# A third buffer for raw weights, and VectorE in place of a DMA for some of the weight rests

## The chip, the cores and the metric

The kernel runs on one core of one Trainium2 chip. The metric is device time in microseconds (us) of one execution. The kernel before takes 2480.88 us, the median of three runs (2478.66 to 2480.95).

## The reference, cut to what matters

Two blocks of two layers each, in float32, on 512 tokens of 1024 features. The first block mixes tokens with differential attention and a gated linear recurrence, then has a feed-forward part (1024 to 4096 and back) and a gated projection of a second input. The second block mixes with pooling and an attention that keeps the 128 best keys by an index score, and then has a feed-forward part with a norm before and behind it:

```
h = rms_norm_2(x, g_pre_ffn[l])
f = jnp.square(jax.nn.relu(h @ w_ff1[l])) @ w_ff2[l]
x = x + rms_norm_2(f, g_post_ffn[l])
```

All weights come from HBM, each is used once. Most of the time goes into products of activations with weights.

## The kernel before, in words

**Split operands.** TensorE multiplies a rounded float type (`F32R`). To keep float32's accuracy each operand is split into a rounded part (the high part, `wh` for a weight) and the rest (`wl` = raw - `wh`), and each product becomes three: high by high, high by rest, rest by high. So a piece of weights passes three stations before TensorE can use it: a load from HBM to a raw tile, a rounding copy to the high tile, and the making of the rest.

**Pieces and their order.** `_plan` lists the pieces of all weights in the order of use. A piece is 128 partitions by 1024 elements, 512 KB: two blocks of 128 rows by 512 columns. The index weights come in smaller pieces (`wx`).
- `w_load` (line 185) asks for a `raw` tile and issues the load on SyncE. There are two raw buffers. SyncE has nearly nothing but these loads in its queue; a load waits there until the splits of the piece that had the buffer have read it.
- `w_conv` (line 192) splits the next piece. ScalarE makes the high part (L205). The rest is made in one of three ways. VectorE subtracts (the `else`). POOL subtracts, in two halves (L218: pieces 1 to 3 of the plan, and the index pieces of the second layer). Or ScalarE copies raw with the sign turned (L211) and POOL issues a DMA (L214) that reads the piece from HBM a second time and adds it to what stands in the tile: minus raw, rounded to the tile's type, plus raw. That last way is used for the weights named in `ON_POOL` from the plan's piece 4 on, and for those in `BY_DMA`.
- `w_ahead` (line 225) keeps the splits up to `LC` = 3 pieces ahead of the piece in use. In each turn of its loop it makes one split and then, if the load counter is less than `LD - LC` ahead of the split counter, one load. `take` calls it before each piece is used.

Piece 0 is split in halves ahead of all this. The high and rest tiles have four buffers each (`wh`, `wl`), which TensorE gives back piece by piece.

**Kept pieces.** In the second block some pieces are used more than once, by `gemm_h`, which works on the two halves of the tokens (256 each) one behind the other so that the norm of the first half can start early. Such pieces are put in tiles of their own by `keep_in`, in the pool `F` of 16 tiles that the feed-forward part also uses for its 16 hidden activations `Fs`. Two sets matter here. At the start of the part, the four pieces of `w_ff1_2` with columns 0 to 511 go into tiles that are free. At its end, the last product (`w_ff2_2`, columns 512 to 1023, rows from 2048 on) does its first 8 row blocks for both halves at once; the other 8, the four pieces k = 24, 26, 28 and 30, are kept for both halves, and their eight tiles are those of the hidden activations that TensorE has just finished with. Both sets are in `BY_DMA`.

**What sets the order.** Each engine works through its own list in order. The lists are planned before the run: program order is the priority, parts marked `urgent` go first, and an instruction is listed when the planner expects its inputs and a free tile. At run time semaphores hold an instruction until both are there, and everything behind it on that engine waits too. TensorE's list is written out by hand in program order. Its instructions and VectorE's pass through the wrapper `Lane`, so all of them show as line L130. Where the second block's norms begin, TensorE has a small product `ones` by `acc` (L130), which sums squares over features. ScalarE's squares (L420) and VectorE's or POOL's adds into `acc` feed it. POOL computes the inverse root (L406), and `bcast` (L444) spreads it.

**Scratch.** `dynamic_dma_scratch_size` sets aside 8 KB of each partition for the descriptors of POOL's DMAs.

The lines that the prediction's steps touch are these: L190 (loads), L205, L211, L214, L218 and the `else` of `w_conv` (splits), `hooks` in `block2` and `mlp` (norms), and `scales` in `mix1` (the first norm's inverse root `v`, on POOL).

Of the kernel before, what the change touches and what calls it, by code (L numbers as in the profile page):

```python
# [8 lines left out]
F32 = mybir.dt.float32  # L9
F32R = mybir.dt.float32r  # L10
# [15 lines left out]
PC = 1024  # L26
ORDER = {"w_out": (4, 5, 6, 7, 0, 1, 2, 3), "w_out_2": (2, 3, 0, 1, 4, 5, 6, 7)}
NX = 11
# [2 lines left out]

URGENT = 250

LD, LC, LH = 4, 3, 4
IDX_SCALE = 8 ** -0.5
ALL = slice(0, 512)
HALVES = (slice(0, 256), slice(256, 512))
# [21 lines left out]
def _plan():  # L59

    plan = []

    def grp(name, l, n0, k0, nk, step, w):
        for k in range(k0, k0 + nk, step):
            plan.append((name, l, n0, k, step, w))

    def mlp(a, b, l):
        for half in range(2):
            for g in range(4):
                grp(a, l, half * 2048 + g * 512, 0, 8, 2, 512)  # L70
            for g in range(2):
                grp(b, l, g * 512, half * 16, 16, 2, 512)

    for l in range(DEPTH):
        for n0 in (1536, 0, 512, 1024):
            grp("w_in", l, n0, 0, 8, 2, 512)
        for n0 in (2048, 2304):
            grp("w_in", l, n0, 0, 8, 4, 256)
        for n0 in range(0, D, 512):
            grp("w_out", l, n0, 0, 4, 2, 512)  # L80
        for g in range(2):
            grp("w_out", l, g * 512, 4, 4, 2, 512)
        mlp("w_mlp_in", "w_mlp_out", l)
        for g in range(2):
            grp("w_ple_proj", l, g * 512, 0, 2, 2, 512)
            grp("w_ple_gate", l, g * 512, 0, 8, 2, 512)
    for l in range(DEPTH):

        for k0, nk in ((0, 4), (4, 4)) if l == 0 else [(k, 2) for k in range(0, 8, 2)]:
            for n0, w in ((0, 256), (256, 328)):  # L90
                grp("index", l, n0, k0, nk, 2, w)
        for n0 in (512, 1024, 1536):
            grp("w_in_2", l, n0, 0, 8, 2, 512)
        for n0 in (256, 0):
            grp("w_in_2", l, n0, 0, 8, 4, 256)
        for n0 in range(0, D, 512):
            grp("w_out_2", l, n0, 0, 4, 2, 512)
        for g in range(2):
            grp("w_out_2", l, g * 512, 4, 4, 2, 512)
        mlp("w_ff1_2", "w_ff2_2", l)  # L100
    return plan


PLAN = _plan()

BY_DMA = [e for e in PLAN if e[0] == "w_ff1_2" and e[2] in (0, 512) or e[0] == "w_ff2_2" and e[2] == 512 and e[3] >= 24]
ON_POOL = ("w_in", "index", "w_in_2", "w_out", "w_out_2")


# [1 line left out]
def two_blocks_kernel(ctx: ExitStack, tc: tile.TileContext, io):  # L111
    nc = tc.nc
    V, A, G, SY = nc.vector, nc.scalar, nc.gpsimd, nc.sync

    def behind(r, last):

        tc.add_manual_dep(r.ins, last.name, mybir.DependencyInfo(
            mybir.DependencyClass.NoSync, mybir.DependencyReason.DATA), reason="issue order")

    class Lane:  # L120


        def __init__(self, eng, on=False, last=None):
            self.eng, self.on, self.last = eng, on, last
# [18 lines left out]
    xp = ctx.enter_context(tc.tile_pool(name="acts", bufs=1))  # L143
# [8 lines left out]
    class Tags:  # L152
# [5 lines left out]
        def __call__(self, tag, dt=None, shape=None):  # L158
# [1 line left out]
            return self.pool.tile(shape or sh, dt or d, name=nm(tag), tag=tag, bufs=n)  # L160

    C512 = [128, 512]
    P = Tags(xp, X=([128, 2, 512], F32R, NX), raw=([128, PC], F32, 2), wh=([128, PC], F32R, 4),
             wl=([128, PC], F32R, 4), sn=([128, 8], F32, 4), v4=([128, 4], F32, 4), ri=([128, 4], I32, 2),
             rh=([128, 4], F32, 2), rt=([128, 4], F32, 2), rs=([128, 4], F32, 3), acc=(C512, F32, 2),
             mn=([128, 1], F32, 6), sm=([128, 4], F32, 6), sq=([128, 8], F32, 3), iw=([128, 8], F32, 4),
# [18 lines left out]
    def w_load():  # L185
        i = st["ld"]
        st["ld"] += 1
        n = PLAN[i][4] * PLAN[i][5]
        raws[i] = P("raw")
        SY.dma_start(raws[i][:, :n], where[i])  # L190

    def w_conv():
        i = st["cv"]
        st["cv"] += 1
        n = PLAN[i][4] * PLAN[i][5]
        r = raws.pop(i)
        h_, l_ = keep[PLAN[i]]() if PLAN[i] in keep else (P("wh"), P("wl"))
        if i == 0:
            for a in range(0, n, n // 2):
                b = slice(a, a + n // 2)  # L200
                A.activation(h_[:, b], r[:, b], AF.Copy)
                V.tensor_sub(l_[:, b], r[:, b], h_[:, b].bitcast(F32))
            his[i], los[i] = h_, l_
            return
        g = A.activation(h_[:, :n], r[:, :n], AF.Copy)  # L205
        if "bcast" in st:
            behind(g, st["bcast"].ins)
        if (PLAN[i][0] in ON_POOL and PLAN[i][0] != "index" and i > 3
                and PLAN[i][:4] != ("w_in_2", 0, 512, 0)) or PLAN[i] in BY_DMA:

            g = A.activation(l_[:, :n], r[:, :n], AF.Copy, scale=-1.0)  # L211
            if "bcast" in st:
                behind(g, st["bcast"].ins)
            G.dma_start(l_[:, :n], where[i], accum_op=OP.add)  # L214
        elif PLAN[i][0] == "index" and PLAN[i][1] == 1 or i <= 3:
            for a in range(0, n, n // 2):
                b = slice(a, a + n // 2)
                g = G.tensor_sub(l_[:, b], r[:, b], h_[:, b].bitcast(F32))  # L218
                if "rsqrt" in st:
                    behind(g, st["rsqrt"].ins)  # L220
        else:
            V.tensor_sub(l_[:, :n], r[:, :n], h_[:, :n].bitcast(F32))
        his[i], los[i] = h_, l_

    def w_ahead(n=0):
        i = st["i"] + n
        while st["cv"] < len(PLAN) and (st["cv"] <= i + LC or st["cv"] <= i + LH and PLAN[st["cv"]] in keep):
            if st["ld"] <= st["cv"]:
                w_load()
            w_conv()  # L230
            if st["ld"] < min(st["cv"] + LD - LC, len(PLAN)):
                w_load()
# [124 lines left out]
    h = [const.tile([128, S], F32, name=f"h{k}") for k in range(8)]  # L357
    first = P("raw")
    raws[0] = first
# [10 lines left out]
    def col(name, l, i, n=1):  # L370
        o, w = PCOLS[name]
        per = w // DEPTH if name != "g_final" else 0
        return par[:, o + l * per + i:o + l * per + i + n]
# [18 lines left out]
    def split(dst, src, scale=None):  # L392

        if scale is None:
            A.activation(dst[:, 0, :], src, AF.Copy)  # L395
            V.tensor_sub(dst[:, 1, :], src, dst[:, 0, :].bitcast(F32))
        else:
            A.activation(dst[:, 0, :], src, AF.Copy, scale=scale)
            V.scalar_tensor_tensor(dst[:, 1, :], src, scale, dst[:, 0, :].bitcast(F32), op0=OP.mult,
                                   op1=OP.subtract)  # L400
# [7 lines left out]
    class Stat:  # L408


        def __init__(self, tmp):
            self.acc, self.seen, self.tmp = P("acc"), set(), tmp

# [9 lines left out]
        def mean(self, ts=ALL, eps=EPS, scale=1.0 / D):  # L423
# [3 lines left out]
            for t in range(n):  # L427
                a_ = ts.start + t * 128
                PE.matmul(p_[:, t:t + 1], self.acc[:, a_:a_ + 128], ones, start=True, stop=True)
            v_ = P("v4")  # L430
            if isinstance(eps, float):
# [15 lines left out]
    X = [None] * 8  # L447
    with tc.tile_pool(name="start", bufs=1) as sp:
        sq0 = Tags(sp, q=(C512, F32, 2))
        st0 = Stat(lambda: sq0("q"))  # L450
        for k in range(8):
            X[k] = P("X")
            split(X[k], h[k], col("g_mix", 0, k))
            if k == 0:
                w_conv()
        for k in range(8):
            st0.add(h[k])
# [594 lines left out]
    for l in range(DEPTH):  # L1052
        X, fac = block1(l, X, fac, l == DEPTH - 1)
# [466 lines left out]
    for l in range(DEPTH):  # L1520
        X, fac, ahead = block2(l, X, fac, ahead, l == DEPTH - 1)
# [74 lines left out]
```

## Time and profile before

| | |
|---|---|
| runs | 2478.66, 2480.88, 2480.95 us |
| profiled execution | 2476.45 us, span of its instructions 2474.7 us |
| mean granted clock of TensorE | 0.991 of full speed |
| busy: TensorE, VectorE, ScalarE, POOL | 2392.8, 1293.7, 1199.0, 293.8 us |
| loads of raw weights (SyncE) | 379 of 512 KB, median 3.6 us from issue to landing |
| rests by accumulating DMA (POOL) | 107 to `wl`, 16 to `F`, of 512 KB |

In the rows below, a line is an engine, an operation with its tiles (out<-in) and a time in us. The bracket behind it is the time for which that engine was idle just before, and what it waited for. The releaser is inferred from semaphores, and the one named is the one that came last. PE is TensorE, PEld its weight loads, DVE VectorE, ACT ScalarE, SPq SyncE's queue.

### The profile page before, as it was taken

Reading aid. Unit: us, or ns where it says so; the run is one execution under the profiler, and the core shown is the slowest. Engines: PE = TensorE matmul, PEld = TensorE weight load, DVE = VectorE, ACT = ScalarE, POOL = GpSimd, SP = SyncE. Lnnn points to the kernel's source line nnn. Section 1 sums busy time; section 2 is a strip of 40 time slices with the busy share of each in tenths; the row PEclk is TensorE's granted clock in tenths of the full one; section 3 lists DMA queues with packets and bytes.
Section 4 is the critical chain, followed back from the end, with each engine's and each line's share of the span. In section 5 each row is a group of like instructions: output and inputs, shape, how many; then the busy total and the mean of one; then the engine's idle time right before and its main releaser. Section 6 shows DMA issues by size and latency. Waiting matters only on the chain.

```text
span 2474.7 us, 30947 instructions
## 1 busy us (share of the span) xinstructions
PE 2392.8 (97%) x11708; PEld 1989.8 (80%) x11708; DVE 1293.7 (52%) x2532; ACT 1199.0 (48%) x2047; POOL 293.8 (12%) x513
## 2 busy tenths in 40 slices
PE   9999999999999999999999989999989998999997
PEld 6778888888877888888888788888887778888886
DVE  6586433435558543343579755324336975532433
ACT  7785322324678541232465874323236587422331
POOL 2320000000131000000023221000033322100001
PEclk9999999999999999999999999999999999999998
DMA  7743322322874423223257463332345736322323
GB/s 202 170 103 107 98 94 94 101 95 87 187 168 96 114 91 102 94 94 94 82 131 172 90 157 86 94 94 94 102 103 120 170 86 154 94 94 94 101 95 86
DMA packets 80214, 277.70 MB, mean 112 GB/s; under 512 B 9024, under 2 KB 11456, under 8 KB 80064
## 3 DMA queue, kind: packets, MB, share of 16 engines
q1 hardware_dynamic: 62352, 211.22, 27.1%
q0 software_dynamic: 17712, 64.50, 15.2%
q8 instruction: 92, 1.51, 0.2%
q14 instruction: 58, 0.48, 0.1%
HBM read 273.59 MB, written 2.10 MB: 111 GB/s over the span
## 4 chain that ended last, share of the span: by engine, by line
PE 77%; DVE 10%; ACT 8%; issue 2%; DMA 2%; POOL 1%; SPq 0%; DVEq 0%; ACTq 0%; POOLq 0%
PE B L130 77%; ACT xe L668 2%; DVE fo L130 1%; DVE ac L130 1%; DVE X L130 1%; DMA raw<-in_w 1%; DVE m L130 1%; DVE xe L130 1%; ACT wh L205 1%; DVE rn L130 1%; ACT wl L211 1%; DVE pt L130 1%; ACT xe L1284 1%; DVE h L130 1%; DVE acc L130 1%
## 5 line engine op out<-in xcount | busy, mean ns | idle before, releaser
L130 PE MATMUL B<-X,wh 128*128 128x512 f32 (+1 forms) x3200 | 973.1, 387 | 0.0
L205 ACT ACTIVATE wh<-raw 128x1024 fp32r<-128x1024 f32 (+2 forms) x374 | 391.1, 1046 | 826.7 <-PE B L130 803.0
L130 DVE TENSOR_TENSOR wl<-raw,wh 128x1024 fp32r<-128x1024 f32 (+1 forms) x263 | 318.5, 1212 | 745.4 <-ACT wh L205 741.0
L130 PEld LDWEIGHTS B<-X,wh 128*128 128x128 f32 x3200 | 580.6, 189 | 104.0 <-issue 4.3
L130 PE MATMUL B<-X,wl 128*128 128x512 f32 (+1 forms) x1600 | 612.7, 383 | 2.8 <-DMA wl<-in_w 1.8
L130 PE MATMUL B<-F,wh 128*128 128x512 f32 (+1 forms) x2048 | 608.7, 381 | 0.0
L130 PEld LDWEIGHTS B<-F,wh 128*128 128x128 f32 x2048 | 375.8, 188 | 81.8
L130 PE MATMUL B<-F,wl 128*128 128x512 f32 (+1 forms) x1024 | 390.0, 381 | 0.0
L130 PEld LDWEIGHTS B<-X,wl 128*128 128x128 f32 x1600 | 302.3, 189 | 63.4 <-DMA wl<-in_w 2.2
L130 PE MATMUL B<-wh,X 128*128 128x512 f32 (+2 forms) x960 | 291.8, 380 | 0.7 <-DVE X L130 0.7
L130 PEld LDWEIGHTS B<-F,wl 128*128 128x128 f32 x1024 | 192.3, 188 | 40.9
L130 PEld LDWEIGHTS B<-wh,X 128*128 128x128 f32 x960 | 176.2, 190 | 32.6 <-issue 1.9
L130 PE MATMUL B<-wl,X 128*128 128x512 f32 (+2 forms) x504 | 181.4, 374 | 6.3 <-DMA wl<-in_w 3.1
L214 POOL DMA_DIRECT2D wl<-in_w x107 | 93.7, 876 | 452.3 <-ACT wl L211 339.9
L211 ACT ACTIVATE wl<-raw 128x1024 fp32r<-128x1024 f32 x107 | 112.7, 1053 | 48.5 <-PE B L130 48.4
L130 DVE TENSOR_TENSOR f<-r 128x512 f32<-128x512 f32 (+1 forms) x136 | 88.5, 656 | 65.6 <-ACT r L587 65.5
L587 ACT ACTIVATE r<-B 128x512 f32<-128x512 f32 (+1 forms) x136 | 76.3, 566 | 87.7 <-PE B L130 84.9
L130 PEld LDWEIGHTS B<-wl,X 128*128 128x128 f32 x504 | 93.8, 192 | 23.6 <-DMA wl<-in_w 3.5
L406 POOL TENSOR_TENSOR v<-v,nhalf 128x4 f32<-128x4 f32 (+1 forms) x8 | 7.9, 988 | 777.2 <-DVE v L130 777.1
L214 POOL DMA_DIRECT2D F<-in_w x16 | 13.9, 868 | 651.3 <-ACT F L211 629.7
L130 DVE TENSOR_TENSOR F<-f,F 128x512 fp32r<-128x512 f32 (+1 forms) x136 | 89.3, 661 | 1.3 <-ACT F L395 1.0
L130 PE MATMUL B<-ks,qs 128*128 128x256 f32 (+2 forms) x352 | 83.9, 333 | 4.3 <-DVE qs L130 1.8
(216 smaller groups left out, 2503.6 us busy)
## 6 DMA issues: line engine op xcount, KB each, us to landing
raw<-in_w SPq DMA_DIRECT2D x379, 512.0 KB, 3.6
wl<-in_w POOLq DMA_DIRECT2D x107, 512.0 KB, 7.8
F<-in_w POOLq DMA_DIRECT2D x16, 512.0 KB, 7.9
raw<-in_wx SPq DMA_DIRECT2D x8, 328.0 KB, 2.9
h<-in_xT SPq DMA_DIRECT2D x8, 256.0 KB, 5.7
raw<-in_wx SPq DMA_DIRECT2D x8, 256.0 KB, 2.7
out<-h SPq DMA_DIRECT2D x16, 128.0 KB, 1.8
pt<-in_gates SPq DMA_DIRECT2D x2, 512.0 KB, 5.1
```

The lines of the kernel that those rows point to most:

```text
L130: r = f(*a, **k)
L205: g = A.activation(h_[:, :n], r[:, :n], AF.Copy)
L211: g = A.activation(l_[:, :n], r[:, :n], AF.Copy, scale=-1.0)
L214: G.dma_start(l_[:, :n], where[i], accum_op=OP.add)
L406: st["rsqrt"] = G.tensor_tensor(y, v, nhalf[:, :y.shape[-1]], op=OP.pow)
L587: A.activation(r_[:, :n], p_, AF.Relu)
L668: A.activation(e[:, :n], e[:, :n], AF.Exp, scale=-1.0, bias=mn, accum_out=sums)
L1284: A.activation(e[:, :n], e[:, :n], AF.Copy, scale=sm[:, 1:2])
```

## The change

There are three raw buffers where there were two. `LD` goes from 4 to 5. The kept pieces of `w_ff2_2` leave `BY_DMA`, so `w_conv` takes the `else` for them and VectorE subtracts. The bounds for the first pieces go from 3 to 2: piece 3 leaves POOL's subtraction and takes the copy on ScalarE and the accumulating DMA. The scratch goes from 8 KB to 4 KB of each partition, as much as the third raw buffer takes.

```diff
-LD, LC, LH = 4, 3, 4
+LD, LC, LH = 5, 3, 4
...
-BY_DMA = [e for e in PLAN if e[0] == "w_ff1_2" and e[2] in (0, 512) or e[0] == "w_ff2_2" and e[2] == 512 and e[3] >= 24]
+BY_DMA = [e for e in PLAN if e[0] == "w_ff1_2" and e[2] in (0, 512)]
...
-    P = Tags(xp, X=([128, 2, 512], F32R, NX), raw=([128, PC], F32, 2), wh=([128, PC], F32R, 4),
+    P = Tags(xp, X=([128, 2, 512], F32R, NX), raw=([128, PC], F32, 3), wh=([128, PC], F32R, 4),
...
-        if (PLAN[i][0] in ON_POOL and PLAN[i][0] != "index" and i > 3
+        if (PLAN[i][0] in ON_POOL and PLAN[i][0] != "index" and i > 2
                 and PLAN[i][:4] != ("w_in_2", 0, 512, 0)) or PLAN[i] in BY_DMA:
...
-        elif PLAN[i][0] == "index" and PLAN[i][1] == 1 or i <= 3:
+        elif PLAN[i][0] == "index" and PLAN[i][1] == 1 or i <= 2:
...
-    nc = _bacc.Bacc("TRN2", target_bir_lowering=False, num_devices=1, dynamic_dma_scratch_size=8192)
+    nc = _bacc.Bacc("TRN2", target_bir_lowering=False, num_devices=1, dynamic_dma_scratch_size=4096)
```

## Rows read from the trace of the kernel before

**Rows 1.** The page, part 1: each engine's busy time, share of the span, instructions.

```profile
PE 2392.8 (97%) x11708; PEld 1989.8 (80%) x11708; DVE 1293.7 (52%) x2532; ACT 1199.0 (48%) x2047; POOL 293.8 (12%) x513
```

**Rows 2.** TensorE's waits: for whom, us in total, times, the longest.

```profile
PE B L130 <- DVE acc L130: 10.8, 4, 3.9
...
PE B L130 <- DMA F<-in_w: 6.7, 2, 3.9
```

**Rows 3.** Timelines, last product of the second layer: start, us, instruction, idle before.

```profile
2430.14 4.71 PE L130 MATMUL B<-F,F 128*128 128x256 f32 x38
2437.64 3.61 PE L130 MATMUL B<-F,F 128*128 128x256 f32 x17 [2.79 <-DMA F<-in_w]
...
2430.33 1.06 ACT L211 ACTIVATE F<-raw 128x1024 fp32r<-128x1024 f32 x1 [1.79 <-PE B L130]
...
2432.01 0.86 POOL L214 DMA_DIRECT2D F<-in_w  x1 [5.15 <-ACT F L211]
...
2440.18 0.76 DVE L130 TENSOR_TENSOR fo<-B,fo 128x256 f32<-128x256 f32 x2 [28.81 <-PE B L130]
```

**Rows 4.** The timeline of TensorE, last product of the first layer.

```profile
1825.35 4.87 PE L130 MATMUL B<-F,F 128*128 128x256 f32 x26 [3.93 <-DMA F<-in_w]
```

**Rows 5.** Windows: stretch, length, busy of five engines, granted clock, DMA share, GB/s.

```profile
1826.20:1829.70 3.50, 3.50 (x19) 3.50 (x18) 1.60 (x4) 0.75 (x2) 0.00 (x0) 0.51 0.36 116
2437.20:2440.70 3.50, 3.06 (x14) 3.06 (x15) 0.52 (x2) 0.01 (x1) 0.00 (x0) 0.51 0.02 5
```

**Rows 6.** Groups by form (busy, mean ns | idle before); landing of F's DMAs; loads' landing.

```profile
L130 DVE TENSOR_TENSOR wl<-raw,wh 128x1024 fp32r<-128x1024 f32 x253 | 309.4, 1223 | 735.1 <-ACT wh L205 734.9
...
DMA to landing us min/median/max: 5.3/7.9/10.2
...
raw<-in_w SPq DMA_DIRECT2D x379, 512.0 KB, 3.6
```

**Rows 7.** Chain that ended last, and timelines, first layer, `w_out_2` to `w_ff1_2`.

```profile
1451.25 7.96 DMA raw<-in_w
...
1461.58 0.95 DVE L130 TENSOR_TENSOR acc<-acc,q 128x256 f32<-128x256 f32 x2 [4.45 <-ACT q L420]
...
1466.49 0.58 PE L130 MATMUL B<-ones,acc 128*128 128x1 f32 x4 [2.96 <-DVE acc L130]
```

**Rows 8.** The same place in the second layer.

```profile
2070.59 1.06 ACT L205 ACTIVATE F<-raw 128x1024 fp32r<-128x1024 f32 x1 [2.07 <-DMA raw<-in_w]
...
2067.94 9.98 DMA raw<-in_w
...
2081.38 0.58 PE L130 MATMUL B<-ones,acc 128*128 128x1 f32 x4 [3.94 <-DVE acc L130]
```

**Rows 9.** Windows before and in the burst of the first layer (columns as above).

```profile
1440.00:1446.40 6.40, 4.21 (x26) 3.09 (x25) 2.20 (x7) 6.40 (x15) 0.00 (x0) 1.00 0.59 121
1451.20:1459.20 8.00, 6.96 (x58) 6.75 (x58) 3.36 (x9) 3.14 (x7) 1.72 (x2) 1.00 0.91 215
```

**Rows 10.** Timelines of the start: TensorE, ScalarE, POOL.

```profile
27.24 0.39 PE L130 MATMUL B<-X,wl 128*128 128x512 f32 x1
...
36.22 0.50 PE L130 MATMUL B<-wl,X 128*128 128x512 f32 x1 [3.12 <-DMA wl<-in_w]
...
25.87 1.06 ACT L205 ACTIVATE wh<-raw 128x1024 fp32r<-128x1024 f32 x1 [5.35 <-DMA raw<-in_w]
...
22.43 2.53 POOL L218 TENSOR_TENSOR wl<-raw,wh 128x512 fp32r<-128x512 f32 x2
27.28 1.02 POOL L406 TENSOR_TENSOR v<-v,nhalf 128x4 f32<-128x4 f32 x1 [2.31 <-DVE v L130]
28.26 1.06 POOL L214 DMA_DIRECT2D wl<-in_w  x1
```

**Rows 11.** ScalarE's longest wait; the longest later wait of TensorE in the first-layer burst.

```profile
ACT wh L205 <- PE B L130: 803.0, 209, 5.3
...
1498.43 1.78 PE L130 MATMUL B<-X,F 128*128 128x256 f32 x7 [1.55 <-DVE X L130]
```

## The prediction

> **What bounds the kernel now.** I read the busy times first. TensorE is busy 2392.8 of a 2474.7 us span [rows 1], so about 82 us is left to win, and the change leaves every product as it is: anything it gains must come out of TensorE's waits. So the second view is the list of those waits. Two of its entries touch what the change edits: 10.8 us in four waits for VectorE's `acc`, and 6.7 us in two waits for the DMA that finishes an `F` rest [rows 2]. The reader is to see how small they are: no wait on a raw load stands there by itself. The third view is the timeline and the chain around each wait, since a load that is late for ScalarE shows up on TensorE under another name. The last is the granted clock just behind each wait.
>
> **Part 1: the rests of the kept pieces of the last product.** In the last pass the four pieces k = 24, 26, 28, 30 lie in `F` tiles that TensorE gives up only as it ends the first half of the sum. In the second layer the tile for the last rest comes free at 2430.33, ScalarE writes -raw there, POOL issues the accumulating DMA at 2432.01, and TensorE, at work on the earlier kept pieces since 2430.14, stops for 2.79 us until it lands and goes on at 2437.64 [rows 3]. The first layer has the same stop, 3.93 us until 1825.35 [rows 4].
>
> The change puts a `tensor_sub` on VectorE there: 1.22 us, the mean of the 253 such rests that it already does [rows 6]. It can start when the tile is free, 2430.33, and ends near 2431.6. TensorE asks for the rest at 2437.64 - 2.79 = 2434.85, which leaves 3.3 us of cover. VectorE has the time: it is idle for 28.81 us before 2440.18 [rows 3], and nothing stands behind the subtraction until that eviction. What goes off the queues is eight ScalarE copies of 1.06 us, eight POOL issues of 0.86 us [rows 3] and eight accumulating DMAs of 7.9 us [rows 6]; eight subtractions, 9.8 us in all, come onto VectorE. None of this is on the path but the two stops: 3.93 + 2.79 = 6.7 us.
>
> Behind each stop the granted clock is 0.51 for 3.5 us, the lower of the two levels, where TensorE had been idle for three to four microseconds just before [rows 5]. At the full level those 3.5 us hold as much work as 1.7 us would. Behind both stops the next evictions wait on TensorE, so this comes back too if the stop goes: 3.4 us for both. I take it: 3.93 + 1.7 = 5.6 and 2.79 + 1.7 = 4.5, 10.1 us together. Ends: 6.7 (the clock falls anyway) and 10.1. A loss is excluded, since the subtraction would have to be 3.3 us late on an idle engine.
>
> **Part 2: the third raw buffer.** In the code the new `LD` does nothing: each turn of `w_ahead` makes one split and at most one load, so the load counter stays exactly one ahead, with 4 or with 5. But SyncE's loads wait for nothing but their buffer, so a third buffer by itself lets each load leave one split earlier. In steady running that is worth nothing: the first half of a split waits for TensorE to free a `wh` slot, 803.0 us in 209 waits [rows 11], while a load lands in 3.6 us [rows 6].
>
> It counts where splits come in a burst: at the start of the second block's feed-forward part, where the four pieces kept of `w_ff1_2` go into free tiles. First layer: the load that leaves at 1451.25 lands 7.96 us later; ScalarE waits for it in order, and so do the squares for the norm behind it; VectorE's adds come late for the same reason (1461.58, after 4.45 us idle), again for the fourth piece, and TensorE's `ones` product waits 2.96 us until 1466.49 [rows 7]. With three buffers the load that leaves at 1451.25 is already the fourth piece's. By the same row it lands at 1459.2; its split takes 2.1 us, then squares and adds end 1.3 us later (1461.2 to 1462.5 [rows 7]), so near 1462.6. TensorE gets there at 1466.49 - 2.96 = 1463.5. The wait goes, with 0.9 us to spare: 3.0 us.
>
> Second layer: the fourth piece's load takes 9.98 us from 2067.94 and the `ones` product waits 3.94 us. The load before it landed at 2070.59, where ScalarE takes it up [rows 8]; with three buffers the fourth piece's load has that place in the queue, and even with 4 us more its split would end before TensorE needs the adds. 3.9 us. Here I don't count the clock: VectorE's chain of residual and norm follows, TensorE waits on it again up to 1.55 us [rows 11], and a faster stretch would run into that. Ends for the two together: 0, if the loads land no sooner, and 6.9 + 3.4 = 10.3.
>
> What speaks against it is the DMA engines' share: 0.91 over 1451.2 to 1459.2, where loads and accumulating DMAs share them, against 0.59 in the 6.4 us before [rows 9]. A load that leaves earlier uses the room before the burst, so I take the gain. The Trainium skill's page "DMA: Bandwidth & Descriptors", section "Issuing engines are not separate DMA queues", says that DMAs of all engines run on the same 16 engines and interleave, and the share of 0.91 agrees. Taken alone it would leave the burst as long as it is and the sum at the first rival's below; by the row of the room before, the sum is mine.
>
> **Part 3: the start.** The fifth piece (`i` = 4) is late today: its raw buffer is held by the third piece's rest, ScalarE waits 5.35 us for the load, POOL issues the rest at 28.26, behind `v`, and TensorE waits 3.12 us until 36.22 [rows 10]. With three buffers its load leaves after the second piece's rest and that wait goes. But the fourth piece's rest moves from POOL's 2.53 us subtraction at 22.43 to a DMA, and TensorE wants it at 27.24 [rows 10]. POOL is on the third piece's rest until 22.4 (the next starts with no idle time), so the DMA leaves at 22.4 and lands 5.3 (the fastest) to 7.9 us (the median [rows 6]) later, at 27.7 to 30.3. So a new wait of 0.5 to 3.1 us, middle 1.8, stands in for 3.12: I take a gain of 1.3. Ends: 4.8 (no wait, and the clock's 1.7 with it), and a loss of 5.9 if POOL's list puts this DMA behind `v` too: issue at 28.26, landing near 36.2, and TensorE reaches the fifth piece's rest 33.10 - 27.24 = 5.9 us after that.
>
> **Part 4: the scratch.** Halved, it pays for the buffer. The trace doesn't show how full it is: a POOL issue takes 0.86 us, and the idle time before it is put down to ScalarE [rows 3], not to room that was missing. So I take zero; the other end stands with the third rival.
>
> **Sum.** 10.1 + 3.0 + 3.9 + 1.3 = 18.3 us off. The profiled execution took 2476.45 (its span 2474.7 and 1.7 around it), which is 4.4 under the median of the runs, 2480.88. 2476.45 - 18.3 is 2458.2; on the runs' scale it is 2480.9 - 18.3 = 2462.6.
>
> **Rivals.**
> 1. *Only the kept rests gain.* The burst moves as many bytes through engines already 0.91 busy; the loads leave earlier and land when they did, and the start trades one wait for another. 10.1 off: 2470.8. For it: the share [rows 9]. Against it: the room before. Chance 0.15.
> 2. *The start loses.* The fourth piece's rest ends up behind `v` on POOL: 18.3 - 1.3 - 5.9 = 11.1 off, 2469.8. For it: POOL is in order, and today's first such DMA stands behind `v` [rows 10]. Against it: its split is due well before. Chance 0.08.
> 3. *Slower: the order of ScalarE.* The lists are planned ahead, and a raw piece that is there sooner can be listed sooner. A split listed ahead of a softmax step holds that step until TensorE frees a slot, 803.0 / 209 = 3.8 us each by [rows 11]. The place is the four attention stages; it decides from the fifth such split on (18.3 / 3.8), and three in each stage make 12 x 3.8 - 18.3 = 27 us slower, 2508. A scratch that holds POOL back would have the same sign: with one DMA in flight at a time, over a hundred issues would stand 7.9 us apart. Against both: in steady running loads wait for nothing today, so the plan there has no reason to move. Chance 0.06.
> 4. *It doesn't do what it says:* "two ahead" is steered by nothing in the code, the third buffer's loads could gain only where ScalarE is held by something else, and small shifts in the lists eat the 10.1: within 5 us of now, about 2480. Chance 0.07.
>
> My forecast has 0.64. About 0.2% (5 us) is what a measurement of this kernel can tell from no change. Faster by more: 0.64 + 0.15 + 0.08 = 0.87. Within it: the fourth rival's 0.07. Slower: the third's 0.06, and 0.01 out of my own share for several shifts at once, which leaves 0.86 faster and 0.07 slower. The range: the sum with all upper ends is 10.1 + 10.3 + 4.8 = 25.2, or 2455.7; the two rivals that are still faster lie at 2470 and 2471. With the runs' own spread of 2 us at both ends: 2454 to 2473, which leaves out the last two rivals and little more.
>
> **What would show it.** Eight `F` rests on VectorE of 1.2 us, eight `F` DMAs where there were sixteen, and no TensorE wait on a DMA to `F`, with the clock at its full level behind both places: part 1. No wait of ScalarE for raw in either burst, and the `ones` products there without 2.96 and 3.94 us ahead of them: part 2. A short wait on the fourth piece's rest near 27 us and none on the fifth's: part 3. POOL's issues near 0.86 us without new idle time ahead: part 4. I am wrong if the `ones` products still wait with raw there in time, if TensorE has new waits over 3 us elsewhere, or if splits stand ahead of softmax steps.

## The result, and the profile after

The changed kernel takes 2452.99 us (median of 4 runs, 2452.36 to 2456.19), the kernel before 2479.77 in the same runs (4, 2476.85 to 2480.95): ratio 0.9896, 95% interval 0.9879 to 0.9913. It is faster, as forecast, but by 26.8 us where 18.3 were forecast; the time lies 1.0 us below the lower end of the range. The profiled execution took 2452.81 (span 2451.0), 23.6 less than that of before. In the rows POOL is GpSimd.

Both kernels issue the same 11708 products in the same order, so the start of the same product in both traces says what each stage gave. That is the first thing to read here, ahead of any wait:

| up to this product | before | after | after minus before | change in this stage |
|---|---|---|---|---|
| end of the start (`B<-rn,pt`) | 76.63 | 80.05 | +3.42 | +3.42 |
| first `w_ff1_2` burst begins | 1453.08 | 1456.93 | +3.85 | +0.43 |
| behind its `ones` product | 1475.07 | 1474.23 | -0.84 | -4.69 |
| next piece (`B<-X,wl`) | 1510.18 | 1507.91 | -2.27 | -1.43 |
| last product of the first layer begins | 1816.70 | 1814.43 | -2.27 | 0.00 |
| 107th of its 120 `F,F` products | 1835.09 | 1827.14 | -7.95 | -5.68 |
| index stage done (`B<-ks,qs`) | 1906.62 | 1893.46 | -13.16 | -5.21 |
| second `w_ff1_2` burst begins | 2067.01 | 2053.92 | -13.09 | +0.07 |
| behind its `ones` product | 2090.05 | 2070.80 | -19.25 | -6.16 |
| last product of the second layer begins | 2430.01 | 2410.81 | -19.20 | +0.05 |
| its last `F,F` product | 2458.04 | 2434.49 | -23.55 | -4.35 |

How far such offsets can be trusted shows in two other profiles. The kernel with the scratch alone (below) has the instruction lists of the kernel before on every engine, and its stages differ from those of before by up to 2.8 us (start -2.06, up to the first burst +2.77, the two last products +1.34 and -1.91, index stage -0.94, bursts -0.09 and +0.99). A second profile of the changed kernel gives +3.52 at the start, -4.99 and -5.65 for the bursts, -5.67 and -4.35 for the last products and -5.22 for the index stage. So the five gains stand clear of what one profile of a kernel can differ from another, and each is good to a microsecond or two.

Forecast were 5.6 and 4.5 for the two last products (5.68 and 4.35 measured), 3.0 and 3.9 for the bursts (4.69 and 6.16), 0 for the index stage (5.21) and a gain of 1.3 at the start (a loss of 3.42).

The page's busy times and TensorE's waits after (for whom, us in total, times, the longest):

```profile
PE 2382.1 (97%) x11708; PEld 1979.7 (81%) x11708; DVE 1302.0 (53%) x2540; ACT 1191.7 (49%) x2040; POOL 287.5 (12%) x504
```

```profile
PE B L130 <- DMA wl<-in_w: 6.3, 3, 5.0
...
PE B L130 <- DVE acc L130: 2.4, 2, 2.0
```

Against [rows 1] TensorE's busy time is 10.7 us lower for the same products: that part of the gain is clock, not idle time. Against [rows 2] the waits for `F` are gone, those for `acc` fell from 10.8 to 2.4, and one wait of 5.0 us for a `wl` is new.

**Last products.** VectorE's timeline in the second layer, TensorE's beside it, and VectorE's in the first layer:

```profile
2411.19 1.22 DVE L130 TENSOR_TENSOR F<-raw,F 128x1024 fp32r<-128x1024 f32 x1 [4.47 <-PE B L130]
2416.89 0.76 DVE L130 TENSOR_TENSOR fo<-B,fo 128x256 f32<-128x256 f32 x2 [4.47 <-PE B L130]
```

```profile
2419.81 5.68 PE L130 MATMUL B<-F,F 128*128 128x256 f32 x46
```

```profile
1814.68 1.39 DVE L130 TENSOR_TENSOR F<-raw,F 128x1024 fp32r<-128x1024 f32 x1 [4.07 <-ACT wh L205]
```

Each rest takes 1.2 to 1.4 us, is followed by idle time, and TensorE's group of `F,F` products has no wait ahead of it, where [rows 3, 4] had 2.79 and 3.93. The eight `F` DMAs that are left, those of `w_ff1_2`, land in 10.9 us in the median, where the sixteen of [rows 6] took 7.9 and the same eight among them 8.3. TensorE waits for none of them (DMA issues: KB each, median us to landing):

```profile
raw<-in_w SPq DMA_DIRECT2D x379, 512.0 KB, 3.5
wl<-in_w POOLq DMA_DIRECT2D x108, 512.0 KB, 7.7
F<-in_w POOLq DMA_DIRECT2D x8, 512.0 KB, 10.9
```

Windows at the places of [rows 5], at the first burst and at the start (columns as there):

```profile
1463.00:1466.50 3.50, 3.50 (x31) 3.50 (x30) 1.61 (x4) 1.15 (x3) 0.86 (x1) 1.00 1.06 275
1820.00:1823.50 3.50, 3.50 (x31) 3.50 (x31) 1.60 (x4) 0.75 (x2) 0.00 (x0) 1.00 0.10 38
2412.00:2415.50 3.50, 3.50 (x32) 3.50 (x31) 0.41 (x1) 0.00 (x0) 0.00 (x0) 1.00 0.02 5
31.40:38.20 6.80, 5.51 (x15) 4.45 (x16) 0.00 (x0) 2.00 (x2) 0.86 (x1) 0.50 1.04 254
```

The clock is at its full level where it was 0.51 before, and at half behind the new wait at the start.

**First burst.** ScalarE's last kept split, TensorE's `ones` product, and the DMA share:

```profile
1461.40 1.05 ACT L205 ACTIVATE F<-raw 128x1024 fp32r<-128x1024 f32 x1
```

```profile
1467.23 0.50 PE L130 MATMUL B<-ones,acc 128*128 128x1 f32 x4
```

```profile
1454.80:1462.80 8.00, 6.96 (x59) 6.76 (x58) 4.22 (x11) 7.36 (x13) 2.60 (x3) 1.00 0.92 205
```

ScalarE waits for no raw piece, and the `ones` product has no wait where [rows 7] had 2.96. The DMA share in the burst is 0.92, as in [rows 9]: the engines are as full as they were, the fourth load only has an earlier place. Every engine's list is the same as before in both bursts, so nothing but the time of the loads has changed there. ScalarE's busy time in those 8 us went from 3.14 to 7.36.

### The profile page after: what moved, and what is told of

It reads as the page before. It is cut to its first block, busy times and chain, and to the rows that moved or that the text cites. A ratio compares the mean times of both kernels' runs of the same rounds, so it can differ in the third digit from the quotient of the medians.

```text
span 2451.0 us, 30941 instructions
## 1 busy us (share of the span) xinstructions
PE 2382.1 (97%) x11708; PEld 1979.7 (81%) x11708; DVE 1302.0 (53%) x2540; ACT 1191.7 (49%) x2040; POOL 287.5 (12%) x504
## 4 chain that ended last, share of the span: by engine, by line
PE 76%; DVE 12%; ACT 8%; issue 2%; DMA 1%; POOL 0%; SPq 0%; DVEq 0%; ACTq 0%; POOLq 0%
PE B L130 76%; DVE ac L130 2%; DVE m L130 2%; ACT xe L668 1%; DVE fo L130 1%; ACT wh L205 1%; DVE rn L130 1%; ACT wl L211 1%; DVE xe L130 1%; DVE X L130 1%; DMA wl<-in_w 1%; ACT xe L1284 1%; DMA pt<-in_lamk 1%; DVE h L130 1%; DVE pt L130 1%
## 5 line engine op out<-in xcount | busy, mean ns | idle before, releaser
L395 ACT ACTIVATE F<-f 128x512 fp32r<-128x512 f32 (+1 forms) x136 | 81.2, 603 | 3.8 <-DVE f L130 1.7
## 6 DMA issues: line engine op xcount, KB each, us to landing
F<-in_w POOLq DMA_DIRECT2D x8, 512.0 KB, 10.9
```

## Experiments: each part alone

The theory from the two traces (A in the expectations): each part pays in its own stage. Every kernel ran in 5 rounds beside the kernel before.

**The kept rests alone**, two raw buffers and 8 KB scratch left:

```diff
-BY_DMA = [e for e in PLAN if e[0] == "w_ff1_2" and e[2] in (0, 512) or e[0] == "w_ff2_2" and e[2] == 512 and e[3] >= 24]
+BY_DMA = [e for e in PLAN if e[0] == "w_ff1_2" and e[2] in (0, 512)]
```

> The kernel before with one edit: the kept pieces of w_ff2_2 get their rests from VectorE. The changed kernel won 12.3 us around the last product of the first layer and the index product behind it, where I had 5.6, and 4.3 in the second layer. Theory A: the 6.7 us beyond the forecast come from the third buffer (the index weights are there sooner), so this kernel has about 5.6 + 4.4 = 10 us less than before, near 2470, and TensorE's waits of 1.8 and 3.0 us in the index product, with the two clock steps there, are still to be seen. Rival B: they come from the rests themselves, since everything behind the stop starts sooner: 12.3 + 4.3 = 16.6 us less, near 2463, with those two clock steps gone.

Measured: 2468.16 us (6 runs), before 2478.68; ratio 0.9954 (0.9942 to 0.9967), near theory A's 2470. The two last products gave 5.68 and 4.35 by the offsets, the same as with the whole change. The wait for `acc` in the bursts stayed (3.20 us at 1468.00), and two stops of 2.9 us and two half-clock steps stand in the index stage.

**The third buffer alone**, with the 4 KB scratch that makes room for it:

```diff
-    P = Tags(xp, X=([128, 2, 512], F32R, NX), raw=([128, PC], F32, 2), wh=([128, PC], F32R, 4),
+    P = Tags(xp, X=([128, 2, 512], F32R, NX), raw=([128, PC], F32, 3), wh=([128, PC], F32R, 4),
...
-    nc = _bacc.Bacc("TRN2", target_bir_lowering=False, num_devices=1, dynamic_dma_scratch_size=8192)
+    nc = _bacc.Bacc("TRN2", target_bir_lowering=False, num_devices=1, dynamic_dma_scratch_size=4096)
```

> The kernel before with three raw buffers and 4 KB of scratch, and nothing else: pieces 1 to 3 on POOL, the kept rests of w_ff2_2 by DMA. Both theories: the two bursts give 4.7 + 6.1 = 10.8 us as in the changed kernel, and the start gives up to 4.8 (no wait on the fifth piece, no clock step) in place of the 3.5 us that the changed kernel loses there. Theory A: the index product gives 6.7 on top, 22 us in all, near 2458. Rival B: it gives nothing there: 15.6 us, near 2464, and the stops of 3.9 and 2.8 us on the F rests stay under both.

Measured: 2466.26 us (6 runs), before 2478.68; ratio 0.9947 (0.9936 to 0.9958), a gain of 12.4, less than either theory expected (2458 and 2464). By the offsets: bursts -4.98 and -5.92 and index stage -5.07, as theory A has it, but start +2.61, and a loss of 2.66 at the last product of the first layer, where the stop on `F` is longer. TensorE there, and in the kernel with the scratch alone (next experiment), which has two buffers:

```profile
1823.70 6.48 PE L130 MATMUL B<-F,F 128*128 128x256 f32 x30 [5.46 <-DMA F<-in_w]
```

```profile
1825.57 4.70 PE L130 MATMUL B<-F,F 128*128 128x256 f32 x22 [4.96 <-DMA F<-in_w]
```

The stop is 5.46 with the buffer alone, 3.93 in [rows 4], and 4.96 with the lists of the kernel before in another execution; in the second layer it is 2.29 with the buffer alone against 2.79. So it is not shown that the third buffer makes this stop worse. The rests on VectorE take it away in either case.

**The scratch alone** (the line of `dynamic_dma_scratch_size`, and `LD = 5`, which alters no engine's list):

> The kernel before with 4 KB of scratch and LD = 5 and nothing else; its instruction lists are those of the kernel before on every engine. Theory A: 4 KB holds all descriptors that are ever waiting, so the time is that of the kernel before within 2 us and POOL's issues take 0.87 us. Rival B: the smaller ring holds POOL back: slower than before by 3 us or more, with idle time ahead of POOL's DMA issues that ScalarE doesn't explain.

Measured: 2477.02 us (12 runs), before 2478.68; ratio 0.9997 (0.9988 to 1.0006). No cost or gain of either shows, within about 0.1%.

## Experiments: the index stage

With the rests alone the index stage gave 1.03 us, with the buffer alone 5.07. The whole stage in four kernels (columns as in [rows 5]): before, the kept rests alone, the test further below, and the changed kernel:

```profile
1835.09:1906.62 71.53, 63.09 (x393) 57.17 (x391) 46.89 (x113) 41.16 (x84) 30.94 (x40) 0.93 0.46 108
1830.82:1901.32 70.50, 61.35 (x393) 56.06 (x391) 47.04 (x113) 41.03 (x84) 30.48 (x40) 0.95 0.45 109
1831.49:1897.67 66.18, 60.60 (x392) 55.24 (x391) 44.69 (x118) 41.28 (x84) 21.37 (x30) 0.97 0.48 116
1827.14:1893.46 66.32, 59.24 (x392) 53.58 (x391) 47.06 (x113) 41.15 (x84) 30.92 (x40) 1.00 0.48 118
```

From before to after the stage is 5.21 us shorter, and TensorE's busy time alone 3.85: most of the gain shows as clock, and only 1.36 as idle time. GpSimd's timeline in the kernel with the kept rests alone, and TensorE's:

```profile
1852.24 2.11 POOL L218 TENSOR_TENSOR F<-raw,F 128x328 fp32r<-128x328 f32 x2
...
1856.30 0.90 POOL L406 TENSOR_TENSOR rs<-v,nhalf 128x2 f32<-128x2 f32 x1
...
1877.54 0.88 POOL L214 DMA_DIRECT2D wl<-in_w  x1 [4.78 <-ACT wl L211]
...
1878.64 1.01 POOL L406 TENSOR_TENSOR v<-v,nhalf 128x2 f32<-128x2 f32 x1
```

```profile
1857.25 0.43 PE L130 MATMUL B<-ident,rs 128*128 128x128 f32 x2 [2.85 <-POOL rs L406]
...
1881.00 0.58 PE L130 MATMUL B<-ones,acc 128*128 128x1 f32 x4 [2.89 <-ACT ix L1129]
```

and GpSimd's in the changed kernel:

```profile
1844.51 2.13 POOL L218 TENSOR_TENSOR F<-raw,F 128x328 fp32r<-128x328 f32 x2
...
1852.05 0.72 POOL L406 TENSOR_TENSOR rs<-v,nhalf 128x2 f32<-128x2 f32 x1 [1.40 <-DVE v L130]
...
1868.54 0.89 POOL L214 DMA_DIRECT2D wl<-in_w  x1 [0.16 <-issue]
...
1872.42 0.71 POOL L406 TENSOR_TENSOR v<-v,nhalf 128x2 f32<-128x2 f32 x1
```

GpSimd works in order. With two buffers its last subtraction of an index piece ends at 1854.35, and `rs`, which TensorE waits for, stands behind it; with three the subtractions are done at 1846.64 and `rs` waits for VectorE's `v` alone. The list itself is another one: with three buffers the planner puts the later subtractions earlier among the adds into `acc`, and one DMA issue ahead of `rs`. Ahead of `v` stands a DMA's issue; with two buffers GpSimd idles 4.78 us for it, since ScalarE gets that raw piece late:

```profile
1876.18 1.06 ACT L211 ACTIVATE wl<-raw 128x1024 fp32r<-128x1024 f32 x1 [4.65 <-DMA raw<-in_w]
```

SyncE's loads hang on the same list, since a raw buffer is free when GpSimd has read it: the first load behind the index pieces leaves at 1849.13 with the kept rests alone and at 1839.80 in the changed kernel:

```profile
1849.13 5.57 SPq L190 DMA_DIRECT2D raw<-in_w  x2
```

```profile
1839.80 9.99 SPq L190 DMA_DIRECT2D raw<-in_w  x4
```

The profile can't tell whether the late subtraction or the late piece is what counts. The test: the kept rests on VectorE, two buffers, and the subtractions of the second layer's index pieces taken off GpSimd:

```diff
-        elif PLAN[i][0] == "index" and PLAN[i][1] == 1 or i <= 3:
+        elif i <= 3:
```

> The kernel with two raw buffers and the kept rests on VectorE (2468.2 us), in which the rests of the second layer's index pieces go from GpSimd to VectorE too. Theory G (what the third buffer gained in the index stage was GpSimd's list: its subtractions wait for raw pieces that come late, and the statistics `rs` and `v` stand behind them): with the subtractions elsewhere GpSimd makes `rs` and `v` at once, the waits of 2.85 us (ident,rs at 1854) and 2.89 us (the ones product at 1878) fall under 1 us each, with up to two half-clock steps of 1.7 us behind them: 2460 to 2464 us. Rival H (the raw pieces themselves come late, whoever subtracts): TensorE waits for wl or F pieces instead, over 2 us at least twice between 1835 and 1885, and the time stays at 2467 to 2472.

Measured: 2464.75 us (5 runs), before 2478.08; ratio 0.9943 (0.9931 to 0.9956). That is 0.75 over theory G's band and 3.4 below the median with the rests alone (2468.16, measured in other rounds), and the two ratios' intervals overlap, so the traces have to decide. GpSimd, TensorE and ScalarE there:

```profile
1850.05 0.88 POOL L406 TENSOR_TENSOR rs<-v,nhalf 128x2 f32<-128x2 f32 x1
...
1876.63 0.71 POOL L406 TENSOR_TENSOR v<-v,nhalf 128x2 f32<-128x2 f32 x1
```

```profile
1852.30 0.38 PE L130 MATMUL B<-ident,rs 128*128 128x128 f32 x2
...
1878.69 0.58 PE L130 MATMUL B<-ones,acc 128*128 128x1 f32 x4 [0.87 <-ACT ix L1129]
```

```profile
1872.61 1.06 ACT L211 ACTIVATE wl<-raw 128x1024 fp32r<-128x1024 f32 x1 [1.27 <-DMA raw<-in_w]
```

With two buffers the stop of 2.85 us is gone and that of 2.89 is 0.87, TensorE waits for no raw piece, and the stage gives 5.35 us by the offsets (the buffer: 5.07; the whole change: 5.21). For the first stop theory G is shown: of the last three index pieces' loads two leave later than with the rests alone (0.1 and 3.7 us, counted from the stage's first product) and the last 0.4 us earlier, and the stop goes all the same. For the second stop the two causes aren't told apart: the late raw piece there costs ScalarE 1.27 us where it cost 4.65, so with GpSimd's list cleared that piece came sooner too. The two ways win the same 5.1 to 5.4 us by different shares: against the rests alone this one takes 3.6 us of idle time off TensorE and 0.75 of busy time, the third buffer mostly busy time. With the stops gone the stage takes 66.2 to 66.3 us whether TensorE is busy for 59.2 or 60.6 of them.

## Experiments: the start

The new wait stands in the changed kernel's rows of TensorE, GpSimd, SyncE and VectorE:

```profile
32.69 0.80 PE L130 MATMUL B<-X,wl 128*128 128x512 f32 x1 [5.01 <-DMA wl<-in_w]
```

```profile
22.70 1.04 POOL L214 DMA_DIRECT2D wl<-in_w  x1
```

```profile
23.58 0.83 SPq L190 DMA_DIRECT2D raw<-in_w  x2
24.46 0.78 SPq L549 DMA_DIRECT2D pt<-in_lamq  x1
25.29 0.58 SPq L549 DMA_DIRECT2D pt<-in_lamk  x1
```

```profile
40.30 0.42 DVE L130 TENSOR_TENSOR pt<-pt 128x256 f32<-128x256 f32 x1 [13.54 <-DMA pt<-in_lamk]
```

The 4th piece's DMA leaves at 22.70, as the prediction had it (22.4), but TensorE stands until 32.69, 10 us later, where 5.3 to 7.9 were taken from [rows 6], a row that has 10.2 as its longest. And there is a second suspect that no part of the prediction named: VectorE idles 13.54 us until 40.30 for two small loads of the lambda vectors, which SyncE issues behind two raw pieces; the convolution's input stands behind that on VectorE's list.

**The 4th piece back on GpSimd** (the changed kernel with `i > 3` and `i <= 3` as before):

> The changed kernel with one part undone: piece 3 gets its rest from POOL's subtraction again. Theory A: the start's loss is that one DMA, which landed 10 us after its issue and held TensorE for 5.0 us with 6.8 us of half clock behind it; without it there is neither this wait nor the old one of 3.1 us on the fifth piece, so 3.5 + 4.8 = 8.3 us less than the changed kernel, near 2444.5. Rival B: the third buffer's earlier loads crowd the DMA engines at the start, and the fifth piece's rest is as late as before: 3.5 us less at most, near 2449.5, with a wait of about 3 us on wl near 33 us.

Measured: 2456.02 us (4 runs), before 2478.68; ratio 0.9906 (0.9893 to 0.9919). Theory A and rival B both failed: nothing is gained. Its start ends at the same place (76.91 for the end of the last product ahead of the last `B<-rn,pt` group, 76.87 in the changed kernel; the experiments' ends are given at this product, 3.2 us ahead of the table's in the changed kernel), with another wait on the way:

```profile
46.76 3.78 PE L130 MATMUL B<-rn,pt 128*128 128x512 f32 x4 [3.49 <-DVE rn L130]
```

```profile
40.35 0.43 DVE L130 TENSOR_TENSOR pt<-pt 128x256 f32<-128x256 f32 x1 [11.29 <-DMA pt<-in_lamk]
```

**The small loads ahead of the two raw pieces**, nothing else moved in any engine's list:

```diff
         for t_, n in ((lq, "lamq"), (lk, "lamk")):
-            SY.dma_start(t_.rearrange("p a b -> p (a b)"),
-                         bass.AP(tensor=io[n].tensor, offset=io[n].offset, ap=[[0, 128], [1, 256]]))
+            with tc.high_priority(4 * URGENT):
+                SY.dma_start(t_.rearrange("p a b -> p (a b)"),
+                             bass.AP(tensor=io[n].tensor, offset=io[n].offset, ap=[[0, 128], [1, 256]]))
```

> The kernel after, with the two small loads of the lambda vectors (lamq, lamk, 128x256 each) issued on SyncE ahead of the two raw pieces that stand before them; every other engine's list is the same. Theory C (the small loads queue behind raw pieces, VectorE waits for them until 40.3 us and the convolution's input is evicted late): the small loads land by about 32 us, VectorE waits at most for the scale copy at 38.2 us. But the 4th piece's DMA still holds TensorE until 32.7 us, with the half clock behind it, so the start ends at 76.9 us less at most 1 and the time stays at 2453 +- 1.5. Rival D (the small loads are the whole loss of the start): the start ends near 73.4 and the time falls to 2449.5.

Measured: 2456.85 us (4 runs), before 2478.27; ratio 0.9917 (0.9903 to 0.9931). The start ends at 77.37, not earlier; the time is 2.3 over the band of theory C, whose small loads were to land by 32 us, and rival D fell. TensorE, VectorE and ScalarE:

```profile
32.16 0.80 PE L130 MATMUL B<-X,wl 128*128 128x512 f32 x1 [4.52 <-DMA wl<-in_w]
```

```profile
36.16 0.42 DVE L130 TENSOR_TENSOR pt<-pt 128x256 f32<-128x256 f32 x1 [9.42 <-DMA pt<-in_lamk]
41.59 0.69 DVE L130 TENSOR_TENSOR xe<-B,sb 128x512 f32<-128x512 f32 x1 [4.56 <-ACT sb L444]
```

```profile
39.07 1.06 ACT L205 ACTIVATE wh<-raw 128x1024 fp32r<-128x1024 f32 x1 [10.63 <-DMA raw<-in_w]
```

Even ahead of the raw pieces the second small load took 12.1 us to land, until 36.1, beside the two accumulating DMAs that GpSimd had just issued; then a raw piece came late for ScalarE, and the scale `sb` with it.

**Both undone**: the 4th piece on GpSimd and the small loads early.

> Both suspects of the start taken away: the 4th piece's rest is made on GpSimd again, and the small loads go ahead of the two raw pieces. Theory C: the 3.49 us wait of TensorE for the gates at 43.27 us and the half clock behind it (6.8 us, worth 3.4) go, the wait for wl of 1.6 us at 33.4 stays; the start ends near 70 to 73.5 us in place of 76.9, and the time is 2449 (2446 to 2452.5). Rival E (VectorE is late by its own list, the small loads only the last thing it waits for): VectorE then waits for the scale copy until 38.2 or works until about 40, the gates' wait stays over 2.5 us, the start still ends at 76 to 77 and the time is that of the kernel with the 4th piece on GpSimd alone, 2456.

Measured: 2453.15 us (4 runs), before 2478.27; ratio 0.9901 (0.9885 to 0.9916), 0.65 over the expected band. The start does what theory C says:

```profile
29.86 0.43 DVE L130 TENSOR_TENSOR pt<-pt 128x256 f32<-128x256 f32 x1 [1.07 <-DMA pt<-in_lamk]
33.66 0.69 DVE L130 TENSOR_TENSOR xe<-B,sb 128x512 f32<-128x512 f32 x1 [2.92 <-ACT sb L444]
```

The small loads land in 6 us, the gates' wait of 3.49 us is gone, and the start ends at 72.76, 4.1 earlier. The time doesn't show it: it is within the changed kernel's own runs, and in the profiled execution half-clock steps up to the first burst, ahead of the second and behind it, which the changed kernel's doesn't have, take all of it back.

**The 4th piece by DMA with two buffers**, nothing else of the change (`i > 2`, `i <= 2` in the kernel before):

> The kernel before (two raw buffers, 8 KB scratch, kept rests by DMA), with the 4th piece's rest alone moved from GpSimd to a DMA. Theory C (the loss needs the third buffer's loads beside it): the wait for wl of 3.12 us at 33.10 goes or moves to the 4th piece with no more than 3 us, the small loads land by 31 us as before, the start ends at 73.5 +- 1.5 and the time stays at 2478.7 +- 1.5. Rival F (the 4th piece's DMA by itself lands about 10 us after its issue and holds TensorE for 5 us with a half clock of 3.4 behind it): the start ends at 76 to 77 and the time is 2482.

Measured: 2478.98 us (11 runs), before 2478.27; ratio 1.0003 (0.9994 to 1.0012). Its TensorE and VectorE:

```profile
32.43 0.80 PE L130 MATMUL B<-X,wl 128*128 128x512 f32 x1 [4.96 <-DMA wl<-in_w]
```

```profile
34.20 0.42 DVE L130 TENSOR_TENSOR pt<-pt 128x256 f32<-128x256 f32 x1 [7.63 <-DMA pt<-in_lamk]
```

Rival F has the mechanism: the DMA takes 10 us to land with two buffers as well. But the 3.12 us wait of [rows 10] goes in exchange, and the start ends only 2.06 later, within what a time can show. At the table's product the two edits alone are 2.61 later (the buffer) and 2.06 later (the 4th piece's DMA), and together 3.42, 3.52 in a second profile. The sizes of the first two aren't shown: four profiles that have the lists of the kernel before at the start put this product at 74.57 to 77.85, and the two edits at 79.24 and 78.69. What is shown is that the waits lie side by side: with either one undone the other holds the start at about 77, and only with both gone does it end at 72.76 or, below, 71.17.

**The lambda work late.** In place of an earlier load a later use, with the 4th piece on GpSimd:

```diff
-        V.tensor_mul(lq, lq, lk)
...
+        def lam(last):
+            behind(V.tensor_mul(lq, lq, lk), last)
...
             back(0, 1)
+            if l == 0:
+                lam(st["back"])
```

(`st["back"]` is the last scan of the recurrence that `back(0, 1)` issues; the eight instructions behind the product move with it.)

> The kernel after with the 4th piece's rest on GpSimd, and in place of an earlier load a later use: the work on the lambda vectors (one product, one sum, one exponential, six small instructions) is moved on VectorE's list behind the first two scans of the recurrence, some 25 us later; the small loads stay where they were, behind two raw pieces. Theory C: whether the load comes early or the use late is one thing, so the gates' wait at 43.27 us goes as well and the time is 2449 (2446 to 2452.5). If it is not the wait but the traffic of the small loads that costs, this kernel stays at 2456. One table load more on ScalarE (1.3 us) may show beside it, off TensorE's path.

Measured: 2451.79 us (4 runs), before 2478.27; ratio 0.9895 (0.9881 to 0.9909), in theory C's band. `xe` comes at 32.41 with nothing waiting for the lambda loads, which still take 11.9 us to land:

```profile
32.41 0.69 DVE L130 TENSOR_TENSOR xe<-B,sb 128x512 f32<-128x512 f32 x1 [3.76 <-ACT sb L444]
```

The start ends at 71.17, 5.7 us ahead of the changed kernel's. So it was the wait and not the traffic. To compare the two, both ran once more side by side:

> The version with the 4th piece on GpSimd and the lambda work late, once more, now beside the kernel after on the same chip. Its start ended 5.7 us earlier than that of the kernel after, but half-clock steps later in the profiled execution (three more, 1.7 us each) gave most of it back. If those steps are chance, it is 2 to 6 us faster than the kernel after over more runs; if they come with its timing every time, the two are within 2 us (2451.8 against 2453.0).

> The kernel after, unchanged, beside the version above on the same chip: 2453 +- 2 by the runs so far (2452.4 to 2456.2).

Measured: the version 2452.60 us (4 runs, 2448.38 to 2453.13), ratio 0.9887 (0.9870 to 0.9904); the changed kernel 2457.28 (4 runs, 2454.82 to 2457.88), ratio 0.9909 (0.9895 to 0.9922); before 2478.08. The medians are 4.7 us apart and in these runs none of one reaches into the other's, but the intervals of the ratios touch. By its medians it is the fastest kernel of the study. Over both rounds, 8 runs each, the medians are 2452.4 and 2455.5. Whether the half-clock steps are chance stays open: the version's two profiles share those near 776, 1840 and 1959 us and differ in the others, and neither profile of the changed kernel has the first two. The changed kernel itself came out 4.3 us slower than in its first runs, against an expectation of 2453 +- 2; in these runs its time is inside the predicted range. So the times of the three variants of the changed kernel above, 2453 to 2457, can't be told from its own; the profiles carry the argument there.

## Why the forecast was right, and where not

The gain was 26.8 us and not 18.3, and the time fell 1.0 us below the range. Three terms of the sum failed: the clock in the bursts and the index stage, both put at nothing, and the start, which has the wrong sign. The start's error hid part of the other two; that the miss is only 1.0 us is luck. The frame was too narrow as well: "anything it gains must come out of TensorE's waits" stands in the first paragraph, and 10.7 of the 23.6 us are busy time.

**Part 1** was right in mechanism and size: 5.68 and 4.35 against 5.6 and 4.5, the clock's 1.7 behind each stop included, and the same in the kernel that has this edit alone. That they agree to 0.15 us is partly luck, for the kernel with the scratch alone, with the lists of before, has stops of 4.96 and 2.18 there in place of 3.93 and 2.79.

**Part 2, bursts:** the mechanism was right, the size too small. The step that failed is "Here I don't count the clock", a term put at nothing: the half-clock step of 3.4 us behind the first `ones` wait went (4.69 for 2.96 of wait and about 1.6 of clock), and in the second layer 6.16 for 3.94, a half step and a `wl` wait that fell from 0.76 to 0.28. The upper end of that term, 10.3, was nearly the value (10.85). The fear that later waits would swallow it was wrong: `X` is waited for 1.54 us in both kernels, and the offset behind it does not come back.

**Part 2, elsewhere:** the step that failed outright is "In steady running that is worth nothing" outside the bursts. The index stage of the first layer is a third place where late raw pieces hold an in-order engine: GpSimd has `rs` behind its subtractions, and `v` behind a DMA's issue that waits for ScalarE. It gave 5.21, and I had no term for it. The list of waits of the kernel before showed it under the name of ScalarE and VectorE (3.0 us on `ix`, 1.8 on `acc` in that stage), two half-clock stretches of 3.4 and 6.8 us stand there, and the chain wasn't followed.

**Part 3** had the wrong sign. It bounded the 4th piece's DMA by the fastest and the median landing of DMAs late in the kernel, and left out the longest of the same row, 10.2; at the start it took 10 us. The new wait of 5.0 us is one of the signs of being wrong that the prediction names. And it left out that loads without a wait of their own, which the third buffer sends earlier, push back whatever SyncE issues behind them: the second lambda load went from 4.4 us to 14.9, with GpSimd's earlier DMAs beside it. Rival 2 forecast a loss at the start, but by GpSimd's order, and that DMA was not behind `v`.

**Part 4** and the claim that `LD` does nothing were right. Rival 1 fell with the bursts and rival 4 with the buffer's own 12.4. Of rival 3 the price fell: all that lies between the start and the first burst moved by 0.43 us in sum, and between the index stage and the second burst by 0.07. But its premise came true: the plan did move, on ScalarE, VectorE and GpSimd, and most of all in the index stage; how much of the 5.21 us there is the new order isn't shown.

In sum on the profiled executions: 18.3 forecast, +3.95 for the bursts, +5.21 for the index stage, -4.72 for the start, -0.07 for part 1, and +0.9 for the rest (mostly a half-clock step near 1500 that the profiled execution of before has) is 23.6. The median fell by 3.2 more, since the profiled execution of before was 3.3 under the median of its runs and that of after only 0.2.

At the start GpSimd's accumulating DMAs and SyncE's loads slow each other. With two buffers and the 4th piece's DMA as the one edit, that DMA took 9.9 us where the first of the kernel before took 7.9, the raw load behind it 9.3 us where the same load took 4.5, and the second lambda load 9.9 where it took 4.4. A small load ahead of its queue's big ones took 12.1 us with GpSimd's two DMAs issued just ahead of it, and 6.0 where the first of them left 1.2 us behind it. The Trainium skill's page "DMA: Bandwidth & Descriptors", section "Issuing engines are not separate DMA queues", says that DMAs run on the same 16 engines and interleave, whichever engine started them. The trace of the start agrees with it; for the burst the prediction read it as no gain, and the runs had one.

## What to carry to other kernels

A deeper load buffer pays where an in-order engine has something urgent queued behind work on a late piece; look for such places on every engine that touches the pieces (here ScalarE in the bursts and GpSimd in the index stage), and count what TensorE's clock gives back behind each stop that goes. It also sends bulk loads ahead of small ones on the same queue: before deepening it, list what that queue issues behind them and who waits for that. Where an undone edit moves a wait and not the end, two causes lie side by side; undo both before judging either. And profile a kernel with unchanged lists once more: here such a twin differed by up to 2.8 us in a stage, and only larger differences could be read.

## What was not expected of the hardware

The same wait is followed by a half-clock step in one execution and not in the next of the same kernel. TensorE waits 2.25 us for `xe` in both profiled executions of the changed kernel; the windows behind it, in the first:

```profile
1960.50:1963.90 3.40, 3.19 (x17) 2.68 (x18) 1.39 (x5) 2.54 (x7) 0.00 (x0) 1.00 0.24 99
```

and in the second:

```profile
1962.00:1965.40 3.40, 3.21 (x9) 2.58 (x10) 0.80 (x3) 1.45 (x5) 0.00 (x0) 0.50 0.22 88
```

The clock is 1.00 and 0.50, and the second does 9 products where the first does 17 in as much busy time. Such a step costs about 1.5 us by the offsets; the second execution has three that the first hasn't (behind waits at 1262, 1962 and 2098) and its span is 4.7 us longer. All eight timed runs of this kernel lie within 5.5 us of each other, so one to three such steps are of the size of their spread, and a single profile tells little of an edit worth a few microseconds. What decides between the two is left open; no run tested it.

An accumulating DMA of 512 KB into `wl` lands in 7.7 us in the median of the changed kernel, and the 4th piece's in 10 us at the start, with loads beside it, against a median of 3.5 for a plain load of that size.
